# Hybrid decoder step on one core: transposes of short blocks take full 128x128 blocks

## The chip, the cores and the metric

The kernel runs on one core of one Trainium2 chip. The metric is the device time of one execution in microseconds (us), lower is better. Times of engines come from one profiled execution. PE is the tensor engine's matmul side, PEld its weight loads, DVE the vector engine, ACT the scalar engine, POOL GpSimd and SP the queue that issues most DMA transfers.

## What is computed

One layer of a decoder trunk, for a prompt of 1024 positions and for 8 samples of 8 positions each, 1088 rows in all, with 1024 channels, float32:

```python
h = rmsnorm(x, g_norm)
bg_a, cg_a, v_a, z_a, a_b, g_b, z_b, q_x, z_x = split(h @ w_in)        # 3200 columns
conv_a, new_ctx_a = causal_dwconv(ctx_a, cg_a * v_a, w_conv_a, b_conv_a)   # 3 taps, 384 channels
out_a = bg_a * conv_a * silu(z_a)
u_b = a_b * sigmoid(g_b)
conv_b, new_ctx_b = causal_dwconv(ctx_b, u_b, w_conv_b, b_conv_b)          # 31 taps, 384 channels
out_b = silu(layernorm(conv_b, ln_g, ln_b)) * silu(z_b)
out_x = cross_attn(q, mk, mv) * silu(z_x)                                  # 4 heads of 64, 256 memory tokens
y = rmsnorm(x + concat([out_a, out_b, out_x]) @ w_out, g_final)
```

The prompt's memory keys and values come from `rmsnorm(mem) @ w_mem_k` and `w_mem_v`; the samples bring theirs from a cache, and both bring conv states. Outputs are y, the new conv states of both convolutions, and the prompt's keys and values.

## The kernel before

Large products run in three passes of 32-bit matmuls over halves: each operand is split into a high and a low part (`hh`/`hl` for the activations, `wh`/`wl` for a weight tile), and a pass is high x high, low weight x high, high weight x low. The projection goes through 25 column tiles of 128 channels (`n`), each over three chunks of rows of 256, 384 and 448 (`CHUNKS`; the last has 384 rows of the prompt and the 64 of the samples). A pass is eight matmuls, one for each 128 channels of the input (`k`). After the third and the seventh matmul a queue of `steps` is served (`side`), and that is how all the other work of PE (transposes, attention, layer norm) gets between the passes. The taps of the long convolution are DVE instructions, placed behind the evacuations of the passes. Tiles in SBUF come from one pool (`B`), PSUM has four banks for the products (`MM`, names mm) and four for the rest (`SD`, names sd).

Within an engine the order is the order of the program as a scheduler laid it out before the run. The startup is an order written out by hand.

Transposes are PE instructions with the block as weights and the identity `ident` as the other operand; `tr(out, in_, n)` takes a block of n rows and the n x n corner of the identity. The places that the change touches:

- **x** (`x_load`, `x_tr`, `x_T`, `x_ev`): nine row tiles `xt` (names x) are loaded by SP, normalised in place and transposed; the ninth holds the samples and has 64 rows. `x_T(2, k)` makes the third chunk, for each of eight k: three blocks of 128x128 and the samples' block of 64 rows go to one sd bank, and from there ACT writes `hh` and DVE `hl`.
- **parameters and states** (`load_params`, `params_T`): 54 rows of parameters lie in `prow` (names prow), 120 rows of states in each of two `stb`; for each of three groups of channels one block of each is transposed.
- **new states** (`st_out`): 94 columns of `u_s` (names us) and 18 of `s_s` (names ss) are transposed, copied to SBUF and sent out by SP.
- **layer norm** (`ln_in`, `ln_sq`, `ln_scale`, `ln_out`): the convolution's output `accB` is transposed so that a row is a position (`lnx`), normalised, and transposed back; the ninth row tile is again that of the samples: on the way in 64 columns of 128 rows, on the way back 64 rows.
- **the startup**: POOL writes the zeros of `qblk` and then the identity. PE runs 12 matmuls on the identity as a warm-up (line 941, two records each), transposes the norm weights (`graw`, to `gT`), and then the first two row tiles of x, as soon as ACT and DVE have normalised them. ACT makes `hh` from these, piece by piece, and the first pass follows piece by piece, with more matmuls on the identity as fillers (line 972).

Of the kernel before, what the change touches and what calls it, by code (L numbers as in the profile page):

```python
# [11 lines left out]
AF = mybir.ActivationFunctionType  # L12
ALU = mybir.AluOpType
# [6 lines left out]
NS = 64  # L20
NT = SEQ + NS
# [14 lines left out]
def hybrid_trunk_kernel(  # L36
# [7 lines left out]
    nc = tc.nc  # L44
    S, G, T = nc.scalar, nc.gpsimd, nc.tensor
# [13 lines left out]
    V = Vector()  # L59
# [9 lines left out]
    def nm(s):  # L69
        uid[0] += 1  # L70
        return f"{s}_{uid[0]}"

    def B(s, dt=F32, cols=NT):
        return big.tile([128, cols], dt, tag="b", name=nm(s))

    def SD():
        return sdp.tile([128, 512], F32, tag="s", name=nm("sd"))
# [4 lines left out]
    def SM(s, cols):  # L82
        return sml.tile([128, cols], F32, tag=f"{s}{cols}", name=nm(s))

    pe_t, dve_t = [0.0], [0.0]
    steps, taps = deque(), deque()
# [8 lines left out]
    def tr(out, in_, n):  # L95
        T.transpose(out, in_, ident[:n, :n])  # L96
        pe_t[0] += 107

    def dv(ns):
        dve_t[0] += ns  # L100
# [22 lines left out]
        while steps:  # L123
            side()

# [8 lines left out]
    u_s = [cst.tile([128, 334], F32, name=f"us{j}") for j in range(3)]  # L134
# [17 lines left out]
        dv(800)  # L152
        return y0, t3

# [1 line left out]
    hh = [None] * KT  # L156
    hl = [None] * KT
    xt = [None] * 9
    xrows = [128] * 8 + [64]
    xcols = [i * 128 for i in range(9)]  # L160
    groups = [[0, 1], [2, 3, 4], [5, 6, 7, 8]]

    def x_src(i):
        return x_prompt[0, i * 128:(i + 1) * 128, :] if i < 8 else x_sample.rearrange("b t d -> (b t) d")

    def x_load(i):
        xt[i] = B("x", cols=D)
        nc.sync.dma_start(xt[i][:xrows[i]], x_src(i))

    class Norm:  # L170
# [28 lines left out]
    def x_T(c, k):  # L199
        x_ev(c, k, x_tr(c, k))  # L200

    def x_tr(c, k):
        off, n = CHUNKS[c]
        ps = SD()
        for i in groups[c]:
            o, r = xcols[i] - off, xrows[i]
            tr(ps[:, o:o + r], xt[i][:r, k * 128:(k + 1) * 128], r)
        return ps

    def x_ev(c, k, ps):  # L210
# [5 lines left out]
        )  # L216
        dv(n / 0.96 + 130)

# [1 line left out]
    order = (  # L220
        [("g", 0, 15), ("a", 0, 12), ("cg", 0, 3), ("v", 0, 6), ("bg", 0, 0)]
        + [("g", 1, 16), ("a", 1, 13), ("g", 2, 17), ("a", 2, 14)]
# [40 lines left out]
            wlo[n] = B("wl", F32R, D)  # L263
        split(whi[n], wlo[n], raw[n], half * 512, half * 512 + 512)

# [1 line left out]
    u_p = [None] * 3  # L267
    accB = [None] * 3
    W31, WA, BB, BA, LG, LB = 16, 47, 50, 51, 52, 53
# [43 lines left out]
                taps.append(mk(products, 16, 15))  # L313
        taps.append(total)

# [1 line left out]
    sig = [None] * 3  # L317
    s_p = [None] * 3
    cgt = [None]
# [159 lines left out]
        evac(n, c, ps)  # L479
        run_taps(taps_per(n))  # L480

# [1 line left out]
    stb = [None] * 2  # L483
    prw = [None]

    def load_params():
        q = nc.sync
        prow = prw[0] = B("prow", cols=384)
        q.dma_start(prow[0:16, :], state_conv_a[0].rearrange("b p c -> (b p) c"))
        q.dma_start(prow[W31:W31 + 31, :], w_conv_b[0])  # L490
        q.dma_start(prow[WA:WA + 3, :], w_conv_a[0])
        q.dma_start(prow[BB:BB + 1, :], b_conv_b)
        q.dma_start(prow[BA:BA + 1, :], b_conv_a)
        q.dma_start(prow[LG:LG + 1, :], ln_g)
        q.dma_start(prow[LB:LB + 1, :], ln_b)
        for h in range(2):
            stb[h] = B("stb", cols=384)
            q.dma_start(stb[h][:120], state_conv_b[0, 4 * h:4 * h + 4].rearrange("b p c -> (b p) c"))
        G.memset(qblk, 0.0)

    def params_T(j):
        ps = SD()
        cs = slice(j * 128, j * 128 + 128)
        tr(ps[:, 0:54], prw[0][:54, cs], 54)
        tr(ps[:, 64:184], stb[0][:120, cs], 120)
        tr(ps[:, 192:312], stb[1][:120, cs], 120)
        V.tensor_copy(prm[j], ps[:, 0:54])
        V.tensor_copy(
            s_s[j][:, 0:16].rearrange("p (t b) -> p b t", b=NB),
            ps[:, 0:16].rearrange("p (b t) -> p b t", b=NB),  # L510
        )
        for h in range(2):
            V.tensor_copy(
                u_s[j][:, 0:240].rearrange("p (t b) -> p b t", b=NB)[:, 4 * h:4 * h + 4],
                ps[:, 64 + 128 * h:184 + 128 * h].rearrange("p (b t) -> p b t", b=4),
            )
        dv(700)

# [1 line left out]
    mt = [None] * 2  # L520
    mT = {}
    wm = {}
# [86 lines left out]
        V.tensor_sub(KL[0][:, sl], ps, KH[0][:, sl].bitcast(F32))  # L609
        dv(600)  # L610

# [1 line left out]
    P_, PT, mx_, sm_ = {}, {}, {}, {}  # L613

    def at_scores(i):
# [58 lines left out]
    kc, vc, KTs, Os, Pts = {}, {}, {}, {}, {}  # L674

    def c_load(g, p):
# [73 lines left out]
                )  # L750
        dv(500)

# [1 line left out]
    def st_out():  # L754
        tb_ = B("ncb", cols=384)
        ta = B("nca", cols=384)
        ps = SD()
        for j in range(3):
            T.transpose(ps[:94, j * 128:j * 128 + 128], u_s[j][:, 240:334], ident)
        pe_t[0] += 321  # L760
        S.copy(tb_[:94], ps[:94, :384])
        ps = SD()
        for j in range(3):
            T.transpose(ps[:18, j * 128:j * 128 + 128], s_s[j][:, 64:82], ident)
        pe_t[0] += 321
        S.copy(ta[:18], ps[:18, :384])
        for t in range(8):
            nc.sync.dma_start(ncb_s[0, :, 22 + t, :], tb_[t * 8:t * 8 + 8])
        nc.sync.dma_start(ncb_s[0, :, 0:22, :], state_conv_b[0, :, 8:30, :])
        nc.sync.dma_start(ncb_p[0, 0], tb_[64:94])  # L770
        for t in range(2):
            nc.sync.dma_start(nca_s[0, :, t, :], ta[t * 8:t * 8 + 8])
        nc.sync.dma_start(nca_p[0, 0], ta[16:18])

# [1 line left out]
    lnx = {}  # L776
    lst = {}

    def ln_in(i):
        if i == 0:  # L780
            for s in ("sum", "sq"):
                lst[s] = SM(f"ln{s}", 9)
                G.memset(lst[s], 0.0)
        if i % 2 == 0:
            lnx[i // 2] = B("lnx", cols=768)
        r = xrows[i]
        ps = SD()
        for j in range(3):
            T.transpose(ps[:r, j * 128:j * 128 + 128], accB[j][:, i * 128:i * 128 + r], ident)  # L789
        pe_t[0] += 321  # L790
        S.activation(
            lnx[i // 2][:r, (i % 2) * 384:(i % 2) * 384 + 384], ps[:r, :384], AF.Copy,
            accum_out=lst["sum"][:r, i:i + 1],
        )

    def ln_mean():
# [2 lines left out]
        dv(100)  # L799

    def ln_sq(i):
        r = xrows[i]
        t = lnx[i // 2][:r, (i % 2) * 384:(i % 2) * 384 + 384]
        junk = SD()
        S.activation(junk[:r, :384], t, AF.Square, bias=lst["nmu"][:r, i:i + 1], accum_out=lst["sq"][:r, i:i + 1])

    def ln_rstd():
        y0, t3 = rstd_chain(lst["sq"], 9, 384)
# [1 line left out]
        V.tensor_tensor(lst["r"], y0, t3, ALU.mult)  # L810

    def ln_scale(i):
        r = xrows[i]
        t = lnx[i // 2][:r, (i % 2) * 384:(i % 2) * 384 + 384]
        V.tensor_scalar(t, t, lst["nmu"][:r, i:i + 1], lst["r"][:r, i:i + 1], ALU.add, ALU.mult)
        dv(330)

    def ln_out(j, g):
        ps = SD()
        n = 0  # L820
        for i in ((0, 1, 2, 3), (4, 5, 6, 7), (8,))[g]:
            r = xrows[i]
            tr(ps[:, n:n + r], lnx[i // 2][:r, (i % 2) * 384 + j * 128:(i % 2) * 384 + j * 128 + 128], r)
            n += r
        S.activation(
            accB[j][:, g * 512:g * 512 + n], ps[:, :n], AF.Silu,
            bias=prm[j][:, LB:LB + 1], scale=prm[j][:, LG:LG + 1],
        )

# [1 line left out]
    worder = [0, 1, 2, 6, 7, 3, 4, 5]  # L831
    wo_r, wo_h, wo_l = {}, {}, {}

# [86 lines left out]
    def startup():  # L920
# [3 lines left out]
        for i in (0, 1):  # L924
            x_load(i)
# [65 lines left out]
        n2.square(1)  # L991
        evac(2, 0, pr[2])
        t1 = [x_tr(1, k) for k in range(4)]
        pr = [MM(), MM(), MM()]
        for k in range(KT):
# [20 lines left out]
            evac(n, 1, pr[n])  # L1016
        flush_steps()

# [1 line left out]
    if True:  # L1020
        with tc.manual_schedule():
            startup()
        for n in range(0, NCT):
# [8 lines left out]
            kind, j, _ = order[n]  # L1032
# [47 lines left out]
            if n == 17:  # L1080
                ms[0] = B("ms", F32R, D)
                steps.append(st_out)
# [85 lines left out]
```

## Time and profile before

| what | value |
|---|---|
| time, median of 3 runs | 479.92 us (479.91 to 480.08) |
| span of the profiled execution | 479.3 us; its time outside the span is not listed, the median lies 0.6 us above |
| PE busy | 469.2 us, 98%, 2850 instructions |
| PEld busy | 428.5 us, 89% |
| DVE busy | 318.4 us, 66% |
| ACT busy | 221.9 us, 46% |
| POOL busy | 8.1 us, 2% |
| DMA | 40.42 MB, mean 84 GB/s |
| PE on the chain that ended last | 97% |

The busy time of PE includes matmuls whose ends are modelled, and successive ones overlap. A group of the timeline shows the start of its first instruction, the time to the end of its last, the engine, the line, the tiles (written <- read), the shape of the first and the number. The starts of two groups are the safer measure of what lay between.

### The profile page before, as it was taken

How to read it: one execution, taken by the hardware profiler on the slowest of the kernel's cores; microseconds unless marked ns; L12 is line 12 of the kernel's file. 1: busy time of each engine (PE TensorE's matmuls, PEld its weight loads, DVE VectorE, ACT ScalarE, POOL GpSimd, SP SyncE). 2: the span in 40 equal slices, each digit the busy share in tenths (PEclk: the TensorE clock that was granted, in tenths of full speed). 3: DMA queues.
4: the chain of work that ended last, by engine and by line, in shares of the span. 5: the costliest groups of instructions: out<-in, count | busy, mean ns of one | idle time of the engine just before them, and what ended most of it. 6: DMA issues, size and time to landing. Idle time of an engine off the chain costs nothing.

```text
span 479.3 us, 7262 instructions
## 1 busy us (share of the span) xinstructions
PE 469.2 (98%) x2850; PEld 428.5 (89%) x2850; DVE 318.4 (66%) x547; ACT 221.9 (46%) x573; POOL 8.1 (2%) x20
## 2 busy tenths in 40 slices
PE   7999999999999999999999999999999999999994
PEld 6998899999999999999999989899899888888884
DVE  4685599976958899798479598633563446333334
ACT  7874371250215349457592455558852433211111
POOL 2110000000000000000000000000000000000000
PEclk8999999999999999999999999999999999999998
DMA  9970221003440400111020521023401653211111
GB/s 284 353 236 1 89 88 45 0 1 90 130 132 1 133 0 1 46 44 46 2 74 15 176 88 30 17 58 100 166 0 46 189 228 110 87 45 44 45 59 72
DMA packets 39166, 40.42 MB, mean 84 GB/s; under 512 B 1647, under 2 KB 34325, under 8 KB 39125
## 3 DMA queue, kind: packets, MB, share of 16 engines
q1 hardware_dynamic: 39101, 39.96, 26.0%
q8 instruction: 22, 0.36, 0.3%
q14 instruction: 11, 0.09, 0.1%
q10 hardware_dynamic: 32, 0.01, 0.0%
HBM read 34.81 MB, written 5.42 MB: 84 GB/s over the span
## 4 chain that ended last, share of the span: by engine, by line
PE 97%; ACT 1%; DMA 1%; DVE 0%; issue 0%; DVEq 0%; ACTq 0%
PE mm L89 83%; PE sd L89 6%; PE sd L96 6%; DMA x<-in_x_prompt_dram 1%; PE sd L789 1%; ACT junk L180 0%; PE sd L972 0%; PE mm L96 0%; ACT x L191 0%; ACT y L141 0%; DVE yg L53 0%; ACT sd L899 0%; DVEq L1164 0%; DVE xres L53 0%; DVE t L53 0%
## 5 line engine op out<-in xcount | busy, mean ns | idle before, releaser
L89 PE MATMUL mm<-hh,wh 128*128 128x256 f32 (+2 forms) x600 | 119.4, 334 | 0.0
L89 PE MATMUL mm<-hl,wh 128*128 128x256 f32 (+2 forms) x600 | 117.2, 333 | 0.0
L53 DVE SCALAR_TENSOR_TENSOR accB<-u,prm,accB 128x1024 f32<-128x1024 f32 x90 | 115.3, 1282 | 1.5
L89 PE MATMUL mm<-hh,wl 128*128 128x256 f32 (+2 forms) x600 | 115.2, 331 | 0.0
L89 PEld LDWEIGHTS mm<-hh,wh 128*128 128x128 f32 x600 | 98.7, 190 | 4.9 <-issue 1.3
L89 PEld LDWEIGHTS mm<-hl,wh 128*128 128x128 f32 x600 | 97.8, 189 | 5.0 <-issue 1.3
L89 PEld LDWEIGHTS mm<-hh,wl 128*128 128x128 f32 x600 | 98.2, 189 | 4.0 <-issue 0.3
L89 PE MATMUL mm<-wol,mh 128*128 128x512 f32 (+1 forms) x136 | 51.4, 378 | 0.0
L89 PE MATMUL mm<-woh,mh 128*128 128x512 f32 (+1 forms) x136 | 51.3, 377 | 0.0
L89 PE MATMUL mm<-woh,ml 128*128 128x512 f32 (+1 forms) x136 | 51.3, 377 | 0.0
L53 DVE TENSOR_TENSOR xres<-mm,xres 128x512 f32<-128x512 f32 (+2 forms) x19 | 12.5, 662 | 39.8 <-PE mm L89 39.8
L869 ACT ACTIVATE sd<-xres 128x512 f32<-128x512 f32 (+1 forms) x16 | 9.6, 602 | 58.3 <-DVE xres L53 58.3
L53 DVE TENSOR_TENSOR wl<-wr,wh 128x512 fp32r<-128x512 f32 x50 | 33.4, 695 | 4.0 <-ACT wh L243 2.4
L89 PEld LDWEIGHTS mm<-woh,mh 128*128 128x128 f32 x136 | 25.6, 188 | 5.0 <-ACT woh L243 0.4
L89 PEld LDWEIGHTS mm<-wol,mh 128*128 128x128 f32 x136 | 25.6, 188 | 5.0 <-DVE wol L53 0.3
L89 PEld LDWEIGHTS mm<-woh,ml 128*128 128x128 f32 x136 | 25.6, 188 | 4.6
L243 ACT CAST wh<-wr 128x512 fp32r<-128x512 f32 x44 | 25.9, 621 | 0.0
L295 ACT ACTIVATE prod<-us,prm 128x64 f32<-128x64 f32 x93 | 23.6, 341 | 0.0
L636 ACT ACTIVATE P<-sd,nb 128x256 f32<-128x256 f32 x32 | 14.7, 473 | 16.5 <-DVE nb L53 16.4
L438 ACT ACTIVATE sz<-mm 128x256 f32<-128x256 f32 (+2 forms) x24 | 11.3, 472 | 22.9 <-PE mm L89 22.9
L338 ACT ACTIVATE sig<-mm 128x256 f32<-128x256 f32 (+2 forms) x6 | 2.8, 474 | 33.6 <-PE mm L89 33.6
L378 ACT CAST Q<-mm 64x384 fp32r<-64x384 f32 (+1 forms) x12 | 5.3, 439 | 23.6 <-PE mm L89 23.5
(188 smaller groups left out, 518.3 us busy)
## 6 DMA issues: line engine op xcount, KB each, us to landing
wr<-in_w_in_dram SPq DMA_DIRECT2D x25, 512.0 KB
x<-in_x_prompt_dram SPq DMA_DIRECT2D x8, 512.0 KB
wor<-in_w_out_dram SPq DMA_DIRECT2D x8, 512.0 KB
xres<-in_x_prompt_dram SPq DMA_DIRECT2D x8, 512.0 KB
out_dram<-xres SPq DMA_DIRECT2D x7, 512.0 KB
cache<-in_cache_mem_k_dram SPq DMA_DIRECT2D x8, 256.0 KB
cache<-in_cache_mem_v_dram SPq DMA_DIRECT2D x8, 256.0 KB
mem<-in_mem_prompt_dram SPq DMA_DIRECT2D x2, 512.0 KB
```

The source lines that it names most:

```text
L53: r = f(*a, **k)
L89: T.matmul(out, lhsT, rhs, start=start, stop=stop)
L96: T.transpose(out, in_, ident[:n, :n])
L243: S.copy(dst_hi[:, a:b], src[:, a:b])
L295: S.activation(p3[:, k, :], src, AF.Copy, scale=w[:, k0 + k:k0 + k + 1])
L338: S.activation(sig[j][:, off:off + n], ps[:, :n], AF.Sigmoid)
L378: S.copy(q[a, off:off + p], ps[a, :p])
L438: S.activation(sz[0][:, off:off + n], ps[:, :n], AF.Silu)
L636: S.activation(P_[i][:, h * 256:h * 256 + 256], bank[h // 2][:, (h % 2) * 256:(h % 2) * 256 + 256], AF.Exp, bias=nb[:, h:h + 1], scale=SCA ...
L789: T.transpose(ps[:r, j * 128:j * 128 + 128], accB[j][:, i * 128:i * 128 + r], ident)
L869: S.activation(junk[:rows], xr[:rows, cs], AF.Square, accum_out=ss[:rows, f:f + 1])
```

## The change

Every block that is transposed becomes 128 rows by 128 columns. Where there are fewer rows, the rest is zeros that POOL writes: rows 64 to 127 of the ninth x tile, all of prow ahead of its loads, rows 96 to 127 of the two stb tiles. Where there are fewer columns, neighbouring ones are taken: 128 columns of us from 206 on, so that the states stand 34 rows further down, and the last 128 columns of accB, so that the samples stand in rows 64 to 127 of the last layer-norm tile. The 18-column transposes of ss stay as they are, and so does the 16-row one of graw.

```diff
     def x_load(i):
         xt[i] = B("x", cols=D)
+        if xrows[i] < 128:
+            G.memset(xt[i][xrows[i]:], 0.0)
         nc.sync.dma_start(xt[i][:xrows[i]], x_src(i))
...
         for i in groups[c]:
-            o, r = xcols[i] - off, xrows[i]
-            tr(ps[:, o:o + r], xt[i][:r, k * 128:(k + 1) * 128], r)
+            o = xcols[i] - off
+            tr(ps[:, o:o + 128], xt[i][:, k * 128:(k + 1) * 128], 128)
...
         prow = prw[0] = B("prow", cols=384)
+        G.memset(prow, 0.0)
...
             stb[h] = B("stb", cols=384)
+            G.memset(stb[h][96:128], 0.0)
...
-        tr(ps[:, 0:54], prw[0][:54, cs], 54)
-        tr(ps[:, 64:184], stb[0][:120, cs], 120)
-        tr(ps[:, 192:312], stb[1][:120, cs], 120)
+        tr(ps[:, 0:128], prw[0][:, cs], 128)
+        tr(ps[:, 128:256], stb[0][:, cs], 128)
+        tr(ps[:, 256:384], stb[1][:, cs], 128)
...
-            T.transpose(ps[:94, j * 128:j * 128 + 128], u_s[j][:, 240:334], ident)
+            T.transpose(ps[:, j * 128:j * 128 + 128], u_s[j][:, 206:334], ident)
...
+    lncols = [i * 128 for i in range(8)] + [NT - 128]
...
-            T.transpose(ps[:r, j * 128:j * 128 + 128], accB[j][:, i * 128:i * 128 + r], ident)
+            T.transpose(ps[:, j * 128:j * 128 + 128], accB[j][:, lncols[i]:lncols[i] + 128], ident)
...
-        n = 0
-        for i in ((0, 1, 2, 3), (4, 5, 6, 7), (8,))[g]:
-            r = xrows[i]
-            tr(ps[:, n:n + r], lnx[i // 2][:r, (i % 2) * 384 + j * 128:(i % 2) * 384 + j * 128 + 128], r)
-            n += r
+        for n, i in enumerate(((0, 1, 2, 3), (4, 5, 6, 7), (8,))[g]):
+            o = (i % 2) * 384 + j * 128
+            tr(ps[:, n * 128:n * 128 + 128], lnx[i // 2][:, o:o + 128], 128)
+        src = ps if g < 2 else ps[:, 64:128]
+        n = 512 if g < 2 else NS
```

`ln_in`, `ln_sq` and `ln_scale` work on 128 rows of the ninth tile instead of 64, `ln_out` reads its silu's operand from `src`, and `st_out` copies and sends the shifted rows. Comments aside, that is all.

The order on PE is the same but for the shapes and one place below. In the third chunk of x, one group of four transposes (the last is the samples' tile) stands between matmuls of the third pass. Before:

```order
L89 MATMUL mm_396<-hl_148,wh_209 128x384
L96 MATMUL sd_522<-ident,x_108 128x128
L96 MATMUL sd_522<-ident,x_110 128x128
L96 MATMUL sd_522<-ident,x_112 128x128
L96 MATMUL sd_522<-ident,x_114 128x64
L89 MATMUL mm_396<-hl_150,wh_209 128x384
```

After:

```order
L89 MATMUL mm_400<-hl_152,wh_213 128x384
L96 MATMUL sd_526<-ident,x_108 128x128
L96 MATMUL sd_526<-ident,x_110 128x128
L96 MATMUL sd_526<-ident,x_112 128x128
L96 MATMUL sd_526<-ident,x_114 128x128
L89 MATMUL mm_400<-hl_154,wh_213 128x384
```

Nothing moved here; the fourth transpose writes 128 columns instead of 64.

On PE at the layer norm's way back, the transposes of the samples' tile (lnx) for the second and third group of channels stand between matmuls of the projection. Before:

```order
L96 MATMUL sd_3588<-ident,lnx_3417 128x64
L89 MATMUL mm_3638<-hh_155,wh_3440 128x384
L89 MATMUL mm_3638<-hh_141,wl_3441 128x384
L89 MATMUL mm_3638<-hh_143,wl_3441 128x384
L89 MATMUL mm_3638<-hh_145,wl_3441 128x384
L96 MATMUL sd_3591<-ident,lnx_3417 128x64
```

After:

```order
L96 MATMUL sd_3592<-ident,lnx_3421 128x128
L89 MATMUL mm_3642<-hh_159,wh_3444 128x384
L89 MATMUL mm_3642<-hh_145,wl_3445 128x384
L89 MATMUL mm_3642<-hh_147,wl_3445 128x384
L96 MATMUL sd_3595<-ident,lnx_3421 128x128
L89 MATMUL mm_3642<-hh_149,wl_3445 128x384
```

The third transpose moved one matmul ahead.

On POOL at the startup, from the first instruction of the kernel's own on (lnsum and lnsq are the layer norm's sums, ss those of the row norms). Before:

```order
L499 MEMSET qblk 128x512
masks.py:197 MEMSET ident 128x128
L783 MEMSET lnsum_3277 128x9
L783 MEMSET lnsq_3279 128x9
masks.py:199 ISA
masks.py:199 AFFINE_SELECT ident<-ident 128x128
L175 MEMSET ss_174 128x4
```

After:

```order
L789 MEMSET lnsum_3281 128x9
L789 MEMSET lnsq_3283 128x9
L169 MEMSET x_114 64x1024
L491 MEMSET prow_123 128x384
L501 MEMSET stb_132 32x384
L501 MEMSET stb_135 32x384
L503 MEMSET qblk 128x512
masks.py:197 MEMSET ident 128x128
masks.py:199 ISA
masks.py:199 AFFINE_SELECT ident<-ident 128x128
L177 MEMSET ss_178 128x4
```

The four new memsets and the two small ones stand ahead of the identity. On SP the order is the same; the first load into prow and the two loads into stb have POOL among what they wait for.

More of the change, by code (lines that the diff above doesn't have):

```diff
@@ L514, in params_T @@
                 u_s[j][:, 0:240].rearrange("p (t b) -> p b t", b=NB)[:, 4 * h:4 * h + 4],
-                ps[:, 64 + 128 * h:184 + 128 * h].rearrange("p (b t) -> p b t", b=4),
+                ps[:, 128 + 128 * h:248 + 128 * h].rearrange("p (b t) -> p b t", b=4),
             )
@@ L758, in st_out @@
         for j in range(3):
-            T.transpose(ps[:94, j * 128:j * 128 + 128], u_s[j][:, 240:334], ident)
+            T.transpose(ps[:, j * 128:j * 128 + 128], u_s[j][:, 206:334], ident)
         pe_t[0] += 321
-        S.copy(tb_[:94], ps[:94, :384])
+        S.copy(tb_, ps[:, :384])
         ps = SD()
@@ L767, in st_out @@
         for t in range(8):
-            nc.sync.dma_start(ncb_s[0, :, 22 + t, :], tb_[t * 8:t * 8 + 8])
+            nc.sync.dma_start(ncb_s[0, :, 22 + t, :], tb_[34 + t * 8:34 + t * 8 + 8])
         nc.sync.dma_start(ncb_s[0, :, 0:22, :], state_conv_b[0, :, 8:30, :])
-        nc.sync.dma_start(ncb_p[0, 0], tb_[64:94])
+        nc.sync.dma_start(ncb_p[0, 0], tb_[98:128])
         for t in range(2):
@@ L785, in ln_in @@
             lnx[i // 2] = B("lnx", cols=768)
-        r = xrows[i]
         ps = SD()
         for j in range(3):
-            T.transpose(ps[:r, j * 128:j * 128 + 128], accB[j][:, i * 128:i * 128 + r], ident)
+            T.transpose(ps[:, j * 128:j * 128 + 128], accB[j][:, lncols[i]:lncols[i] + 128], ident)
         pe_t[0] += 321
         S.activation(
-            lnx[i // 2][:r, (i % 2) * 384:(i % 2) * 384 + 384], ps[:r, :384], AF.Copy,
-            accum_out=lst["sum"][:r, i:i + 1],
+            lnx[i // 2][:, (i % 2) * 384:(i % 2) * 384 + 384], ps[:, :384], AF.Copy,
+            accum_out=lst["sum"][:, i:i + 1],
         )
@@ L801, in ln_sq @@
     def ln_sq(i):
-        r = xrows[i]
-        t = lnx[i // 2][:r, (i % 2) * 384:(i % 2) * 384 + 384]
+        t = lnx[i // 2][:, (i % 2) * 384:(i % 2) * 384 + 384]
         junk = SD()
-        S.activation(junk[:r, :384], t, AF.Square, bias=lst["nmu"][:r, i:i + 1], accum_out=lst["sq"][:r, i:i + 1])
+        S.activation(junk[:, :384], t, AF.Square, bias=lst["nmu"][:, i:i + 1], accum_out=lst["sq"][:, i:i + 1])
     def ln_rstd():
@@ L812, in ln_scale @@
     def ln_scale(i):
-        r = xrows[i]
-        t = lnx[i // 2][:r, (i % 2) * 384:(i % 2) * 384 + 384]
-        V.tensor_scalar(t, t, lst["nmu"][:r, i:i + 1], lst["r"][:r, i:i + 1], ALU.add, ALU.mult)
+        t = lnx[i // 2][:, (i % 2) * 384:(i % 2) * 384 + 384]
+        V.tensor_scalar(t, t, lst["nmu"][:, i:i + 1], lst["r"][:, i:i + 1], ALU.add, ALU.mult)
         dv(330)
@@ L819, in ln_out @@
         ps = SD()
-        n = 0
-        for i in ((0, 1, 2, 3), (4, 5, 6, 7), (8,))[g]:
-            r = xrows[i]
-            tr(ps[:, n:n + r], lnx[i // 2][:r, (i % 2) * 384 + j * 128:(i % 2) * 384 + j * 128 + 128], r)
-            n += r
+        for n, i in enumerate(((0, 1, 2, 3), (4, 5, 6, 7), (8,))[g]):
[3 more added lines that the diff above has]
+        n = 512 if g < 2 else NS
         S.activation(
-            accB[j][:, g * 512:g * 512 + n], ps[:, :n], AF.Silu,
+            accB[j][:, g * 512:g * 512 + n], src, AF.Silu,
             bias=prm[j][:, LB:LB + 1], scale=prm[j][:, LG:LG + 1],
```

## The prediction

> **What bounds the kernel now.** I read the page first: the busy shares and the chain that ended last.
>
> ```profile
> span 479.3 us, 7262 instructions
> PE 469.2 (98%) x2850; PEld 428.5 (89%) x2850; DVE 318.4 (66%) x547; ACT 221.9 (46%) x573; POOL 8.1 (2%) x20
> PE 97%; ACT 1%; DMA 1%; DVE 0%; issue 0%; DVEq 0%; ACTq 0%
> ```
>
> PE is on the chain for 97% of the span, so whatever PE spends after the first ten microseconds or so counts in full, and nothing that another engine saves counts by itself. A busy PE is not a fast PE, though: a matmul that starts late behind a weight load is still drawn as busy. So I read next the groups kept apart by shape, for the weight loads of the transposes (after the bar: busy us, mean ns of one; then the idle time ahead of them).
>
> ```profile
> L96 PEld LDWEIGHTS sd<-ident,mem 128*128 128x128 f32 x16 | 1.9, 140 | 0.1
> L96 PEld LDWEIGHTS sd<-ident,x 64*128 64x128 f32 x8 | 1.1, 135 | 1.3 <-issue 1.2 <-DVE y L53 0.2
> ```
>
> A load of 64 rows lasts about as long as a full one (135 against 140 ns), but ahead of each stand 0.17 us in which the weight path waits for nothing that the profile shows ("issue"); sixteen full ones have 0.1 us in all. What such a pause costs I take from the timeline of PE: from one row's start to the start of a later one is what PE really spent on the work between.
>
> ```profile
> 24.33 0.49 PE L96 MATMUL sd<-ident,x 128*128 128x128 f32 x3
> 24.58 0.78 PE L89 MATMUL mm<-hh,wh 128*128 128x384 f32 x3
> 25.19 0.49 PE L96 MATMUL sd<-ident,x 128*128 128x128 f32 x3
> ...
> 28.48 4.32 PE L89 MATMUL mm<-hh,wl 128*128 128x384 f32 x24
> 32.63 0.86 PE L89 MATMUL mm<-hl,wh 128*128 128x384 f32 x4
> 33.33 0.69 PE L96 MATMUL sd<-ident,x 128*128 128x128 f32 x4
> ...
> 38.31 1.37 PE L96 MATMUL sd<-ident,x 128*128 128x128 f32 x8
> 39.61 0.97 PE L89 MATMUL mm<-hl,wh 128*128 128x384 f32 x4
> 40.43 0.69 PE L96 MATMUL sd<-ident,x 128*128 128x128 f32 x4
> 41.05 0.97 PE L89 MATMUL mm<-hl,wh 128*128 128x384 f32 x4
> 41.86 0.69 PE L96 MATMUL sd<-ident,x 128*128 128x128 f32 x4
> ```
>
> A 384-column matmul costs (32.63 - 28.48) / 24 = 0.173 us. Three full transposes with three matmuls take 25.19 - 24.33 = 0.86, so 0.34 for the three, 0.11 each and 0.44 for four. Three full blocks and one of 64 rows with four matmuls take 41.86 - 40.43 = 1.43, so 1.43 - 0.69 = 0.74: **0.30 us more with one short block**, although it moves half the columns. (The timeline merges the shapes; the fourth of each x4 is the short one.) Two such groups in a row take 40.43 - 38.31 - 0.69 = 1.43 against 0.88, 0.55 more.
>
> **Samples' rows of x.** Eight groups carry the samples' block: two pairs and four single groups, 2 x 0.55 + 4 x 0.30 = 2.3 us, all on PE, which go if a padded block behaves like the other full ones. What is late next is the bank: four PSUM banks serve the groups, and the fifth needs the first one back from DVE.
>
> ```profile
> 36.59 2.45 DVE L53 SCALAR_TENSOR_TENSOR hl<-sd,gT,hh 128x448 fp32r<-128x448 f32 x4
> ```
>
> Group one starts at 33.33; with 0.44 for a group and 0.69 for the matmuls between (four groups, three sets), the fifth would start at 33.33 + 3.83 = 37.16 and the sixth, right behind, at 37.6. DVE comes to this row from other work without a gap, so PE can't hurry it; one of its four takes 0.61, and banks come free at 37.2 and 37.8. That takes back 0.05 + 0.2: **2.05 us saved**.
>
> **States and parameters.**
>
> ```profile
> 45.12 0.26 PE L96 MATMUL sd<-ident,prow 54*128 54x54 f32 x1
> ...
> 49.49 0.27 PE L96 MATMUL sd<-ident,prow 54*128 54x54 f32 x1
> ...
> 50.78 1.81 PE L89 MATMUL mm<-hh,wl 128*128 128x448 f32 x8
> 52.43 1.81 PE L89 MATMUL mm<-hl,wh 128*128 128x448 f32 x8
> ```
>
> From one group of three transposes to the next stand eight matmuls, which take 52.43 - 50.78 = 1.65. Two rounds last 49.49 - 45.12 = 4.37, so a group costs 4.37 / 2 - 1.65 = 0.53, against 3 x 0.11. Three groups save 3 x 0.2 = **0.6 us**. The loads into prow and stb now wait for POOL's zeros, written by 4 us (below); SP comes to these loads later than that, behind its x, w and mem loads, so nothing behind them in its queue loses time.
>
> **Layer norm, the way back.**
>
> ```profile
> 345.16 0.27 PE L96 MATMUL sd<-ident,lnx 64*128 64x64 f32 x1
> 345.37 0.45 PE L89 MATMUL mm<-hh,wh 128*128 128x384 f32 x1
> 345.65 0.70 PE L89 MATMUL mm<-hh,wl 128*128 128x384 f32 x3
> 346.28 0.27 PE L96 MATMUL sd<-ident,lnx 64*128 64x64 f32 x1
> ```
>
> One 64-row transpose with four matmuls takes 346.28 - 345.16 = 1.12, less 0.69 is 0.43: 0.3 more than a full one; three of them, 0.9. ACT has to give back their banks, and the third now stands one matmul earlier on PE, with ACT busy just then; for that I take off 0.1, half a matmul: **0.8 us saved**.
>
> **Blocks short in columns, not in rows** (the last of accB, 64 columns of 128 rows; the states out, 94 columns).
>
> ```profile
> 325.77 0.49 PE L789 MATMUL sd<-ident,accB 128*128 128x128 f32 x3
> ...
> 327.06 0.49 PE L789 MATMUL sd<-ident,accB 128*64 128x128 f32 x3
> ...
> 328.33 1.55 PE L89 MATMUL mm<-hh,wh 128*128 128x384 f32 x8
> ```
>
> Three full ones and eight matmuls take 1.29, three short ones and eight matmuls 1.27: no pause to remove, 0.02 to lose. The same is assumed for the 94 columns. The wider ACT and DVE instructions cover more partitions with as many elements in each. All of this I cost at **nothing**; it would be hidden by PE anyway, which waits for none of it.
>
> **The start.** This is the cost.
>
> ```profile
> 0.73 0.52 POOL L499 MEMSET qblk<- 128x512 f32 x1 [0.29 <-POOLq L1155]
> 1.19 0.20 POOL masks.py:197 MEMSET ident<- 128x128 f32 x1
> ```
>
> A memset costs 0.83 ns a column and 0.09 us (0.52 for 512, 0.20 for 128). Zeros of 1024, 384, 384 and 384 columns ahead of the identity are 0.95 + 3 x 0.41 = 2.2 us, so PE's warm-up, which waits for the identity, starts near 4.0 instead of 1.85.
>
> ```profile
> 1.85 4.47 PE L941 MATMUL sd<-ident 128*128 128x128 f32 x24 [1.85 <-POOL ss L175]
> ...
> 8.22 0.68 PE L96 MATMUL sd<-ident,x 128*128 128x128 f32 x3 [1.73 <-ACT x L191]
> 8.69 0.85 PE L96 MATMUL mm<-ident,x 128*128 128x128 f32 x3
> 9.33 0.85 PE L96 MATMUL sd<-ident,x 128*128 128x128 f32 x3
> ...
> 13.86 0.36 PE L89 MATMUL mm<-hh,wl 128*128 128x256 f32 x1
> ```
>
> ```profile
> 9.79 1.20 ACT L212 ACTIVATE hh<-sd,gT 128x256 fp32r<-128x256 f32 x3 [0.59 <-PE sd L96]
> ```
>
> ```profile
> 5.08:8.49 3.41, 1.68 (x14) 1.46 (x14) 2.30 (x12) 3.35 (x8) 0.00 (x0) 1.00 1.16 308
> 8.49:11.91 3.42, 3.42 (x19) 3.42 (x17) 3.42 (x8) 2.83 (x8) 1.68 (x2) 0.50 1.13 350
> ```
>
> In the windows (length, then busy times from PE to POOL, then the granted clock) the clock is full from 5.08 to 8.49, and half from 8.49 to 11.91, after a stretch with PE busy for only 1.68 of 3.41 us. If the clock steps at the same places, the late warm-up runs at half clock, (9.33 - 8.69) / 3 = 0.213 a piece, up to 8.49, where 21 of 24 are done, and ends near 8.8; the transpose of g follows and the first x comes near 9.1 instead of 8.2, now without PE's gap of 1.7, so the full clock should stay. The seventh transpose of x, for which ACT waits, then starts at 9.1 + 6 x 0.11 = 9.8 instead of 9.33 and, by the 0.46 from there to ACT's start less what the full clock gains, ACT begins near 10.1 instead of 9.79. Its eight pieces of 0.40 end at 13.3, and PE follows with one matmul and two fillers of about 0.11 each: the second pass starts near 13.8, where it now starts at 13.86, since PE worked off a backlog made at half clock. Bounds: 2.2 lost, if the delay passes through whole; 0.6 gained, ACT's idle time in the row at 9.79, if the clock rises early enough that ACT has nothing to wait for. I take **0.1 lost**: nearest to the row at 13.86, and on the side of a loss, since POOL's memsets may also wait for each other.
>
> The Trainium skill ("TensorE: Matmul & The Clock Gate", Part 1) has the clock decided in free-running windows of about 3.4 us, with half clock after an idle one. The trace agrees on the length (3.41 and 3.42), but here the clock fell after a window that was half busy.
>
> **Sum.** 2.05 + 0.6 + 0.8 - 0.1 = 3.35 us. The profiled span of 479.3 becomes 475.95. The median of the runs, 479.92, lies 0.6 above that span, so the forecast is 476.6. A measurement of this kernel tells about 0.2%, 0.96 us, from no change.
>
> **Rivals.**
>
> A. The start's delay passes through: whole, 3.45 - 2.2 = 1.25 saved, 478.7; half, 2.35 saved, 477.6. For it: PE did wait 1.85 us for POOL. Against it: PE's gap of 1.73 ahead of the first x takes up most of it.
>
> B. Other engines take back gain further on: PE waits for nothing there now, so their margins aren't seen. Half lost, 478.2. Against it: DVE is busy for 66% and ACT for 46%, and what waits for PE moves forward with it.
>
> C. Slower: the late warm-up leaves the clock low. Each further window of 3.4 us at half clock costs PE 1.7; with the 2.2 passing whole, two of them cost 5.6 against 3.45, so 482.1. It is slower from a loss of 4.4 on. Against it: PE no longer has the gap after which the clock fell.
>
> D. The pause isn't made by the missing rows but by the change from one kind of work to another, and stays. Then nothing is saved, and with 0.1 lost the time is 480.0. For it: 135 against 140 ns, rows don't shorten a load. Against it: the mem groups change kind as often and don't pause.
>
> The Trainium skill, same page ("LDWEIGHTS (loading the stationary operand)"), says that a load's time goes by its columns and not by its rows: by that rule alone D holds, and padding can't save anything. The trace agrees for the load itself and shows the pause outside it.
>
> **Chances.** The forecast case 0.72, with its own range from 475.6 (0.6 gained at the start, and 0.3 of the 0.35 taken off for banks doesn't come) to 477.2 (0.7 lost at the start). A 0.11, B 0.09, D 0.04, C 0.04, half of it no change and half slower. Faster by over 0.2% are the forecast, A and B, 0.92; no change D and half of C, 0.06; slower 0.02. The range reaches from 475.5 into A and B, to 478.3; A's upper end, C and D are left out.
>
> **What the profile after would show.** The "issue" ahead of the samples' and parameters' weight loads is gone; the last of the eight groups starts near 40.1 (41.86 now); a parameter group with its eight matmuls takes 1.98 and not 2.19; the warm-up starts near 4.0 and the second pass between 13.7 and 14. The prediction is wrong if the pauses are still there, if the second pass starts after 15, or if DVE or ACT stands as PE's releaser after 40 us with more than 0.5 us.

## The result, and the profile after

| kernel | median, us | lowest to highest | ratio to before |
|---|---|---|---|
| before | 479.92 | 479.79 to 480.08 | 1 |
| after | 477.75 | 476.93 to 478.50 | 0.995 (0.9933 to 0.9966) |

The change saves 2.17 us by the medians, and 1.6 to 3.2 us by the interval. The forecast was 476.6, with 475.5 to 478.3 as its range. The page of after, to set beside the first lines of the prediction:

```profile
span 476.7 us, 7269 instructions
PE 465.8 (98%) x2850; PEld 427.6 (90%) x2850; DVE 318.3 (67%) x547; ACT 221.8 (47%) x573; POOL 10.3 (2%) x24
```

PE executes as many instructions as before and is busy for 3.4 us less; POOL has four memsets and 2.2 us more. This span belongs to an execution of 478.50 us, so 1.8 us lie outside the span. All later profiles have the same 1.8.

The groups of weight loads by shape (after the bar: busy us, mean ns of one; then idle time ahead of them):

```profile
L96 PEld LDWEIGHTS sd<-ident,x 128*128 128x128 f32 x66 | 7.8, 144 | 1.2 <-DVE hl L53 0.7
L96 PEld LDWEIGHTS sd<-ident,prow 128*128 128x128 f32 x3 | 0.4, 139 | 0.0
```

The "issue" is gone from both. What idle time is left ahead of the x loads ends mostly with DVE's `hl`, 0.7 us. Of that 0.5 us lies here, on the timeline of the weight loads:

```profile
38.27 0.42 PEld L96 LDWEIGHTS sd<-ident,x 128*128 128x128 f32 x4 [0.31 <-DVE hl L53]
38.86 0.42 PEld L96 LDWEIGHTS sd<-ident,x 128*128 128x128 f32 x4 [0.17 <-DVE hl L53]
```

These are the fifth and the sixth group, which wait for the banks that the prediction named. On PE's timeline (start, time to the end of the last, engine, line, operation, tiles, shape of the first, count), the third chunk of x and the parameter groups:

```profile
34.26 0.60 PE L96 MATMUL sd<-ident,x 128*128 128x128 f32 x4
34.62 0.95 PE L89 MATMUL mm<-hl,wh 128*128 128x384 f32 x4
...
36.20 0.94 PE L89 MATMUL mm<-hl,wh 128*128 128x384 f32 x4
...
37.34 0.94 PE L89 MATMUL mm<-hl,wh 128*128 128x384 f32 x4
38.27 1.25 PE L96 MATMUL sd<-ident,x 128*128 128x128 f32 x8
39.27 0.94 PE L89 MATMUL mm<-hl,wh 128*128 128x384 f32 x4
40.06 0.60 PE L96 MATMUL sd<-ident,x 128*128 128x128 f32 x4
...
41.19 0.60 PE L96 MATMUL sd<-ident,x 128*128 128x128 f32 x4
41.55 1.87 PE L89 MATMUL mm<-hh,wh 128*128 128x448 f32 x8
...
44.07 0.27 PE L96 MATMUL sd<-ident,prow 128*128 128x128 f32 x1
...
47.98 0.27 PE L96 MATMUL sd<-ident,prow 128*128 128x128 f32 x1
...
49.12 1.78 PE L89 MATMUL mm<-hh,wl 128*128 128x448 f32 x8
50.74 1.78 PE L89 MATMUL mm<-hl,wh 128*128 128x448 f32 x8
```

A single group with its four matmuls takes 41.19 - 40.06 = 1.13 instead of 1.43, and less 0.69 for the matmuls 0.44: the length of four full blocks. Four matmuls and a pair of groups behind them take 36.20 - 34.62 = 1.58 at the second and third group, which wait for no bank, and 39.27 - 37.34 = 1.93 at the fifth and sixth: the banks cost PE 0.35. Two parameter rounds take 47.98 - 44.07 = 3.91, 1.96 each.

What each stage gained, by the starts on PE at its two ends:

| stage | before | after | saved |
|---|---|---|---|
| third chunk of x: first group to the 448-column pass | 33.33 to 42.48 | 34.26 to 41.55 | 1.86 |
| parameters: that pass to the next `mm<-hh,wl` pass | 42.48 to 50.78 | 41.55 to 49.12 | 0.73 |
| states out (us) to the first lnx block on the way back | 312.27 to 339.72 | 310.44 to 337.89 | 0.00 |
| layer norm, way back, to the pass behind it | 339.72 to 347.47 | 337.89 to 344.90 | 0.74 |
| second pass to PE's last matmul | 13.86 to 472.56 | 14.80 to 470.01 | 3.49 |

The last row is what I call the body: 458.70 before, 455.21 after. The 3.49 is the gain behind the start, and the forecast had 3.45.

The four stages above it add up to 3.33. The other 0.16 lies in the five 448-column passes behind the parameters, which hold no transpose: a pass takes 50.74 - 49.12 = 1.62 in after and 52.43 - 50.78 = 1.65 in before (rows in the prediction). The runs below show these two paces and none between: the five passes take 8.27 in before, e2, e5, e8 and e9, and 8.11 in all others. As e6 keeps every short block and has 8.11, and e8 pads x and has 8.27, the 0.16 doesn't follow the pauses. Nothing in the traces says what sets the pace; where bodies are compared below, the 0.16 is named.

The median gained only 2.17. The rest went in the start:

```profile
0.93 0.95 POOL L169 MEMSET x<- 64x1024 f32 x1
1.94 0.42 POOL L491 MEMSET prow<- 128x384 f32 x1
2.42 0.77 POOL L501 MEMSET stb<- 32x384 f32 x2
...
3.71 0.21 POOL masks.py:197 MEMSET ident<- 128x128 f32 x1
4.34 5.49 PE L944 MATMUL sd<-ident 128*128 128x128 f32 x24 [4.34 <-POOL ss L177]
9.97 0.74 PE L96 MATMUL sd<-ident,x 128*128 128x128 f32 x3
...
14.80 1.20 PE L89 MATMUL mm<-hh,wl 128*128 128x256 f32 x8
```

The identity comes after four memsets, the warm-up starts at 4.34 instead of 1.85, and its 24 records take 5.49 us, 0.23 a piece, near the 0.213 that the prediction read at half clock. By the trace's clock records the clock is full from 10.42, and the second pass starts at 14.80. With the predicted 13.8 that is a loss of 1.0, but the runs below show that the row I measured it against, 13.86, was itself not the usual start of before.

The theory after this: short blocks of rows cost a pause, padding removes it, and the zeros cost part of that gain because they stand ahead of the identity. Rivals: the pause belongs to the change of kind of work; a shorter block costs in proportion to its missing rows, or once for each short block; and the lost microsecond is not the zeros' but chance, or the fault of a warm-up that queues ahead of x.

### The profile page after: what moved, and what is told of

Read it like the earlier page. It is cut to its first block, busy times and chain, and to the rows that moved or that the text cites. A ratio compares the mean times of both kernels' runs of the same rounds, so it can differ in the third digit from the quotient of the medians.

```text
span 476.7 us, 7269 instructions
## 1 busy us (share of the span) xinstructions
PE 465.8 (98%) x2850; PEld 427.6 (90%) x2850; DVE 318.3 (67%) x547; ACT 221.8 (47%) x573; POOL 10.3 (2%) x24
## 3 DMA queue, kind: packets, MB, share of 16 engines
q1 hardware_dynamic: 39101, 39.96, 26.7%
## 4 chain that ended last, share of the span: by engine, by line
PE 97%; DVE 1%; POOL 1%; issue 0%; ACT 0%; DVEq 0%; POOLq 0%; ACTq 0%
PE mm L89 83%; PE sd L89 6%; PE sd L96 5%; PE sd L944 1%; PE sd L794 1%; DVE wl L53 0%; PE sd L975 0%; POOL x L169 0%; POOL stb L501 0%; DVE yg L53 0%; ACT sd L902 0%; POOL qblk L503 0%; DVEq L1167 0%; DVE xres L53 0%; POOL prow L491 0%
## 5 line engine op out<-in xcount | busy, mean ns | idle before, releaser
L640 ACT ACTIVATE P<-sd,nb 128x256 f32<-128x256 f32 x32 | 14.8, 473 | 16.5 <-DVE nb L53 16.4
```

Of the source, the lines that this page charges most:

```text
L640: S.activation(P_[i][:, h * 256:h * 256 + 256], bank[h // 2][:, (h % 2) * 256:(h % 2) * 256 + 256], AF.Exp, bias=nb[:, h:h + 1], scale=SCA ...
```

## Experiments

Kernels timed together share their runs of before. Its median was 480.32 beside the first four runs named e1 to e4, 479.91 beside e5 to e9, and 480.43 beside e10 to e12; e5 to e9 ran on another chip than the other experiments. Two profiles of one kernel agree within 0.05 in the body (458.70 and 458.75 before, 455.21 and 455.17 after), so a single profile is enough to read it.

**The gain without the zeros ahead: the identity first (e1).** On the kernel after, in the startup:

```diff
+        make_identity(nc, ident)
         ...
         w_load(4)
-        make_identity(nc, ident)
```

> The changed kernel with the identity written ahead of POOL's zeros; nothing else. Theory (the padded blocks save 3.3 us on PE, the zeros ahead of the identity give about 0.9 back at the start, more or less by where the clock steps): the warm-up starts near 1.5, the second pass (first matmul with a low weight) near 13.8 instead of 14.80, and the time is 476.4 to 476.8, about 1.0 below the changed kernel's 477.75, with a spread of runs below 0.6. Rival (the gain was lost further on, behind 40 us): the start is earlier but the time stays at 477.4 to 478.

Measured: 476.94 (476.27 to 479.48), ratio 0.9937 (0.9918 to 0.9956). The profiled execution has a span of 474.5:

```profile
1.39 5.01 PE L944 MATMUL sd<-ident 128*128 128x128 f32 x24 [1.39 <-POOL ident masks.py:199]
...
12.60 1.19 PE L89 MATMUL mm<-hh,wl 128*128 128x256 f32 x8
```

The second pass starts at 12.60, 2.2 earlier than in after, and the body is 455.19, as in after. In this profile the same zeros, written behind the identity, cost nothing: the second pass starts as early as it does without them in e5 (12.64), though here the warm-up also starts 0.46 earlier than in before. By the times this is less sure, since the interval of the ratio overlaps that of after (0.9933 to 0.9966). The median came out somewhat above what was expected, and the spread of 3.2 far above. Of its six executions the three with a mean granted clock of 0.995 to 0.999 lie at 476.27 to 476.41, and the three with 0.991 to 0.993 at 477.46 to 479.48. In the profiles a mean of 0.993 or 0.994 goes with a clock that fell back to half in the start (the first of before, and e12), and all others have 0.995 or more. So the clock of the start is the likely cause; it is not shown, as the last three left no trace.

**The cost alone: zeros written, blocks left short (e2).** On the kernel before, the four memsets of the change and nothing else:

```diff
+        if xrows[i] < 128:
+            G.memset(xt[i][xrows[i]:], 0.0)
...
+        G.memset(prow, 0.0)
...
+            G.memset(stb[h][96:128], 0.0)
```

> The kernel before with the four memsets of zeros where the change puts them; every transpose stays as it was. Theory: the warm-up starts near 4.3, the clock rises late by an amount that differs from run to run, the time is 480.2 to 481.6, the median about 0.9 above before. Rival A (the delay is hidden by the wait for x): 479.9, second pass at 13.9. Rival C (the clock stays low for whole windows more): above 482.

Measured: 481.55 (480.71 to 481.87), ratio 1.002 (1.0006 to 1.0033): slower by 1.2 us.

```profile
4.34 5.49 PE L945 MATMUL sd<-ident 128*128 128x128 f32 x24 [4.34 <-POOL ss L177]
...
14.50 0.72 PE L89 MATMUL mm<-hh,wl 128*128 128x256 f32 x4
```

The start of after with the body of before: 473.25 (PE's last matmul) - 14.50 = 458.75. The start's loss comes with the zeros, then, whatever the blocks are: 1.2 us by the medians, 0.3 to 1.6 by the interval.

**One part alone: x (e3).** On the kernel before, x in full blocks, with its one memset behind the identity:

```diff
-            o, r = xcols[i] - off, xrows[i]
-            tr(ps[:, o:o + r], xt[i][:r, k * 128:(k + 1) * 128], r)
+            o = xcols[i] - off
+            tr(ps[:, o:o + 128], xt[i][:, k * 128:(k + 1) * 128], 128)
...
+        G.memset(xt[8][64:], 0.0)
```

> The kernel before with the samples' x block padded alone, and its zeros written behind the identity, so that the start stays. Theory (a pause for every block of fewer rows): the eight groups save 1.8 to 2.1 us, 477.9 to 478.1. Rival (the pause comes with the change of work and not with the rows): 479.9.

Measured: 478.42 (477.72 to 479.02), ratio 0.9961 (0.9949 to 0.9972). The stage of the third chunk, from the first group to the 448-column pass:

```profile
32.69 0.60 PE L96 MATMUL sd<-ident,x 128*128 128x128 f32 x4
...
39.96 1.87 PE L89 MATMUL mm<-hh,wh 128*128 128x448 f32 x8
```

It takes 39.96 - 32.69 = 7.27 instead of 9.15 (42.48 - 33.33): 1.88 saved, against 2.05 in the prediction. The body is 456.62, 2.08 less than 458.70, but 0.16 of that is the other pace of the five passes behind the parameters. The time is somewhat above what was expected: the second pass began at 13.21 in the profiled execution.

**Before, once more (e5).** The kernel before without an edit, for a second profile.

> The kernel before, unchanged, for a span and a time of the same execution. Theory (the first profile of before fell on an execution in which the clock dropped for a window, and the time lies 1.8 us above the span as in the other runs): time less span is 1.7 to 1.9; if the clock doesn't drop in this one, the second pass starts at 12.7 to 13.2 and the span is about 478.2; if it does, 13.9 and 479.3. From the second pass's start to the last matmul's it takes 458.7 either way. Rival (the start is always as in the first profile): time less span 0.6, second pass at 13.9, span 479.3.

Measured: 479.90, the median of before.

```profile
span 478.1 us, 7262 instructions
...
8.09 0.55 PE L96 MATMUL sd<-ident,x 128*128 128x128 f32 x3 [1.00 <-ACT x L191]
...
12.64 1.20 PE L89 MATMUL mm<-hh,wl 128*128 128x256 f32 x8
```

The windows of this execution and of the one that the prediction read (length, then busy us and count from PE to POOL, the granted clock, the share and GB/s of DMA):

```profile
9.00:12.00 3.00, 2.98 (x25) 2.55 (x23) 3.00 (x8) 2.95 (x10) 1.38 (x2) 1.00 1.11 356
```

```profile
9.00:12.00 3.00, 3.00 (x16) 3.00 (x15) 3.00 (x7) 2.41 (x7) 1.68 (x2) 0.52 1.12 363
```

With the clock full, the second pass of before starts at 12.64, not at 13.86. This execution is a usual one: of the 17 of before that were timed beside e5 to e9, twelve took 479.84 to 479.93. Other kernels with the same early warm-up and a clock that stayed full have 12.56, 12.79 and 13.21 (e8, e6, e3). The first profile belonged to an execution in which the clock fell back to half; by the 1.8 us outside the span it took 481.1 and not 479.9. Against 12.64 the start of after loses 2.16 in its profile.

**After, once more (e11).** The kernel after without an edit.

> The changed kernel, unchanged, for a second profile. Theory (its start differs from run to run with the place at which the clock steps, the rest doesn't): warm-up at 4.34 again, clock up somewhere between 7 and 10.5, second pass at 13.2 to 14.9, and from there to the last matmul 455.2 as in the first profile. Rival (the spread of 1.6 between its runs lies elsewhere): the second pass within 0.2 of 14.80 and a different time behind it.

Measured: 477.75, and its body 455.17.

```profile
4.34 5.02 PE L944 MATMUL sd<-ident 128*128 128x128 f32 x24 [4.34 <-POOL ss L177]
...
14.09 1.08 PE L89 MATMUL mm<-hh,wl 128*128 128x256 f32 x7
```

The same start at 4.34, but the clock is full from 8.73 instead of 10.42, and the second pass starts at 14.09: 1.45 behind the 12.64 of before. The two profiled executions of after differ in their starts and in nothing behind them.

**A shorter warm-up (e10).** If the late warm-up delays x by standing ahead of it in PE's queue, half as many should help. On the kernel after:

```diff
-    WARM = 12
+    WARM = 6
```

> The changed kernel with 6 warm-up matmuls instead of 12; the zeros stay ahead of the identity. Theory (the delay costs because the late warm-up, at half clock, keeps PE until 9.5 while x is ready at 8): six end near 7, x starts at 8.0 to 8.2, the second pass between 12.6 and 13.9, and the time is 476.3 to 477.5, below the changed kernel's 477.75. Rival (what costs is the clock's late rise, whatever stands in PE's queue): with fewer warm-up matmuls the clock rises later still, the second pass starts at 14 to 15, 477.7 to 478.7.

Measured: 477.95 (477.66 to 478.34), ratio 0.994 (0.9923 to 0.9958). No better than the 477.75 of after beside it.

```profile
4.34 2.93 PE L944 MATMUL sd<-ident 128*128 128x128 f32 x12 [4.34 <-POOL ss L177]
8.13 0.90 PE L96 MATMUL sd<-ident,x 128*128 128x128 f32 x3 [0.64 <-ACT x L193]
...
14.22 0.96 PE L89 MATMUL mm<-hh,wl 128*128 128x256 f32 x6
```

The first x comes at 8.13, as early as in before, so the queue is out of the way. But x then runs at half clock (0.90 for three against 0.55 in e5), the clock is full only from 12.53, and the second pass starts at 14.22. My theory of the queue fell: without the queue the loss stayed. The run changed two things at once, the queue and the place where the clock steps up, so that the late clock is the loss is what fits the starts and not shown by itself.

**A longer warm-up on the early start (e4).** e1 with this:

```diff
-    WARM = 12
+    WARM = 20
```

> The identity first, and 20 warm-up matmuls instead of 12, so that PE has no gap ahead of the first x and the clock doesn't fall again. Theory (the clock falls after a window with PE half busy): the granted clock stays full from its first rise on, the second pass starts at 13.3 to 13.7, and the time is 0.2 to 0.6 below that of the identity first with 12, 475.9 to 476.5. Rival (ACT's pieces set the start, not the clock): the same time as with 12, within 0.2. Against both: if the clock rises late, 20 matmuls end after the first x is ready, and it gets up to 0.5 slower.

Measured: 476.74 (476.44 to 477.11), ratio 0.9926 (0.9914 to 0.9937): the lowest median of all versions, 3.6 us under the before beside it, and with a spread of 0.7 instead of e1's 3.2. Its highest time is below the median of after, though the intervals of the two ratios still touch (0.9914 to 0.9937 and 0.9933 to 0.9966).

```profile
1.39 6.65 PE L944 MATMUL sd<-ident 128*128 128x128 f32 x40 [1.39 <-POOL ident masks.py:199]
8.24 0.55 PE L96 MATMUL sd<-ident,x 128*128 128x128 f32 x3
...
12.79 1.20 PE L89 MATMUL mm<-hh,wl 128*128 128x256 f32 x8
```

The warm-up now ends at 8.04, as x arrives, so PE has no gap there, and the clock stays full, as the theory had it. The second pass starts at 12.79; I had expected 13.3 or later. The time is above the expected 475.9 to 476.5, and 0.2 below e1, which the rival allowed too: the runs don't tell 20 from 12 here by the time.

**The longer warm-up on before (e9).** `WARM = 20` on the kernel before, with the identity where it stood.

> The kernel before with 20 warm-up matmuls instead of 12. Theory (part of before's spread is a clock that drops after the gap ahead of the first x): no drop, the second pass at 12.7 to 13.3, the time 479.8 to 480.4 with a spread below 0.8, so the median stays where it is and the slow executions go. Rival (the drop doesn't matter): same median and the same spread of 1.2 and more.

Measured: 480.72 (479.93 to 481.51), ratio 1.0012 (1.0003 to 1.0022): no gain, rather 0.6 us worse by the ratio, with a spread of 1.6.

```profile
1.85 6.74 PE L941 MATMUL sd<-ident 128*128 128x128 f32 x40 [1.85 <-POOL ss L175]
8.69 0.55 PE L96 MATMUL sd<-ident,x 128*128 128x128 f32 x3
...
13.15 1.20 PE L89 MATMUL mm<-hh,wl 128*128 128x256 f32 x8
```

From 1.85 the forty records end at 8.59, so the first x waits, at 8.69 instead of 8.09, and the second pass starts at 13.15 instead of 12.64. The clock didn't fall back, but the spread stayed, and the median rose: the theory that a longer warm-up helps by itself fell. That it helps beside the earlier identity rests on the spreads of e1 and e4, six and five executions, and isn't shown.

**What makes the pause: each short block, or the change to it (e6).** On the kernel before, each short block of x is transposed twice, one behind the other:

```diff
             tr(ps[:, o:o + r], xt[i][:r, k * 128:(k + 1) * 128], r)
+            if r < 128:
+                tr(ps[:, o:o + r], xt[i][:r, k * 128:(k + 1) * 128], r)
```

> The kernel before with the samples' 64-row transpose of the third chunk issued twice in a row in each of the eight groups. Theory (a pause for every short block): the second one costs 0.20 as the first does, so the work from the second pass on takes 1.6 more, 460.3. Rival (a pause at the change between full and short): the second one costs 0.11, 0.9 more in all, 459.6.

Measured: 480.34 once, body 459.06, 0.36 more than before. The five passes behind the parameters run at the faster pace here and hide 0.16, so the stage itself is the measure:

```profile
32.28 0.75 PE L96 MATMUL sd<-ident,x 128*128 128x128 f32 x5
...
41.93 1.89 PE L89 MATMUL mm<-hh,wh 128*128 128x448 f32 x8
...
L96 PEld LDWEIGHTS sd<-ident,x 64*128 64x128 f32 x16 | 1.6, 137 | 1.3 <-issue 1.2 <-DVE y L53 0.2
```

The last line is from the groups by shape, the others from PE's timeline. The stage takes 41.93 - 32.28 = 9.65 instead of 9.15: 0.06 for each of eight added blocks, below what either theory had (0.20 and 0.11). Sixteen loads have the same 1.2 us of "issue" in all as eight had. The single starts of the last group show where the pause stands. The first short block starts 0.20 behind the full one ahead of it, where full blocks follow each other in 0.11; the second starts 0.11 behind the first. In before, the next matmul starts 0.20 behind the short block, in after 0.03 behind the full one in its place. The theory that every short block pauses fell: the pauses stand at the two changes, into a block of 64 rows and out of it, and a second block of 64 rows behind the first has none ahead of it. The "issue" of the weight path shows only the first of the two; the 0.30 that the prediction read on PE holds both.

**How short is short (e8).** On the kernel before, the samples' block with 96 rows, 32 of them zeros written behind the identity:

```diff
             o, r = xcols[i] - off, xrows[i]
+            r = max(r, 96)
...
+        G.memset(xt[8][64:], 0.0)
```

> The kernel before with the samples' block padded to 96 rows and 96 columns instead of 128 (zeros behind the identity). Theory (every block of fewer than 128 rows pauses): as with 64 rows, 458.7 from the second pass on. Rival (only blocks up to half the rows pause): as with 128 rows, 456.6 as in the run with the x block padded alone.

Measured: 477.91 once. The stage takes 39.34 - 32.03 = 7.31, 1.84 less than before, and the body of 456.86 is 1.84 less too.

```profile
L96 PEld LDWEIGHTS sd<-ident,x 96*128 96x128 f32 x8 | 1.1, 140 | 0.0
...
L96 PEld LDWEIGHTS sd<-ident,prow 54*128 54x128 f32 x3 | 0.4, 135 | 0.9 <-issue 0.9
```

In one kernel, 96 rows have no idle time ahead and 54 rows have 0.3 us each. It isn't "fewer than 128 rows" either: 96 rows do as well as 128, 7.31 against the 7.27 of e3. (The bodies differ by 0.24, of which 0.16 is the pace of the five passes.)

**The parameters alone (e12).** On the kernel before with the identity first, only prow padded; the two blocks of states keep their 120 rows (the identity's move and the copies' new columns are not printed):

```diff
+        G.memset(prow, 0.0)
...
-        tr(ps[:, 0:54], prw[0][:54, cs], 54)
-        tr(ps[:, 64:184], stb[0][:120, cs], 120)
-        tr(ps[:, 192:312], stb[1][:120, cs], 120)
+        tr(ps[:, 0:128], prw[0][:, cs], 128)
+        tr(ps[:, 128:248], stb[0][:120, cs], 120)
+        tr(ps[:, 256:376], stb[1][:120, cs], 120)
...
```

> The kernel before with the block of parameters alone padded, 54 rows to 128 (identity first, zeros behind it); the state blocks keep their 120 rows. Theory (only blocks of up to half the rows pause): all of that group's gain comes, 0.7, so 458.0 from the second pass to the last matmul. Rival (120 rows pause too): half of it or less, 458.4 or more.

Measured: 480.02 once, body 457.85.

```profile
L96 PEld LDWEIGHTS sd<-ident,stb 120*128 120x128 f32 x6 | 0.8, 140 | 0.2
L96 PEld LDWEIGHTS sd<-ident,prow 128*128 128x128 f32 x3 | 0.4, 138 | 0.0
...
42.29 1.90 PE L89 MATMUL mm<-hh,wh 128*128 128x448 f32 x8
...
49.88 1.79 PE L89 MATMUL mm<-hh,wl 128*128 128x448 f32 x8
```

The parameter stage takes 49.88 - 42.29 = 7.59, in after 7.57, before 8.30. All of that stage's gain came from the 54-row block; padding the 120-row blocks of states brought nothing. The body is 0.85 less than before, 0.71 by this stage and the rest by the pace of the five passes. This execution was one in which the clock fell back: full from 5.24 to 8.65, then half to 12.07, and its second pass starts at 13.68, just like the first profile of before.

## Why the prediction was right, and where it wasn't

**Samples' rows of x: right.** Predicted 2.05, measured 1.86 in the stage, and 1.88 for this part alone (e3). The wait for banks is there, at the fifth and sixth groups as predicted; it cost 0.35 where 0.25 was taken off. That the body's 3.49 lies so close to the 3.45 of the forecast is in part luck: 0.16 of it is the pace of five passes, which the prediction didn't have.

**States and parameters: right in size, not in attribution.** Predicted 0.6, measured 0.73. The three blocks of a group were costed together; e12 shows that the 54-row block carries all of it.

**Layer norm: right.** Predicted 0.8, measured 0.74.

**Short columns: right.** Predicted nothing, and the stage from the states out to the way back takes 27.45 us in both kernels.

**The start: mis-sized.** The term was 0.1 lost. Measured are 1.45 and 2.16 in two profiles of after against 12.64, and 3.49 - 2.17 = 1.3 by the medians. (Beside e10 and e11 before has a median of 480.43 and after is 2.7 faster in one execution, which leaves 0.8; e2 has 1.2.) Three things went into it. The row at 13.86 was taken as the usual start of before; it was one with the clock fallen back, and the usual start is 12.64 (e5). The clock was assumed to step up where it did in that profile; after a warm-up from 4.34 it stepped up at 10.42 and 8.73 (10.17 in e2). And the memsets with the gaps between them delayed the warm-up to 4.34, not to 4.0. The warm-up then ended at 9.83 and the first x came at 9.97, against 8.8 and 9.1 in the forecast.

**"The median lies 0.6 above that span": wrong.** Time outside the span is 1.8 us in every run with both numbers. The first profile's span of 479.3 belongs to an execution of 481.1. This error and the one in the start have one cause, a profile taken as typical, and partly cancel: the sum off the span, 475.95, is 0.75 below the profiled 476.7, and with 1.8 instead of 0.6 it would have given 477.75, the measured median, by luck. From the typical profile of before, span 478.1 and second pass at 12.64, the same terms with the start at 13.8 give 478.1 - 3.45 + 1.16 = 475.8, and 477.6 with what lies outside.

**The rivals.** A is what happened, in its half version (477.6): about half of the 2.2 us came through. B did not happen: the body kept its 3.49. C did not happen: the highest time of after is 478.50, and the clock came late but stayed. D was half right in its mechanism and wrong in its result: the pause does stand at a change, but at the change between 64-row and full loads, so full blocks do away with it (e3, e6, e8). The loads themselves last 135 ns with 54 rows, 137 with 64, 140 with 96 and 139 with 128. In this the trace agrees with the rule of the Trainium skill that the prediction set beside D ("TensorE: Matmul & The Clock Gate", "LDWEIGHTS (loading the stationary operand)"); the pause stands outside the load, where that rule says nothing.

**What the profile after was to show.** The "issue" is gone; a parameter round takes 1.96 (forecast 1.98). The last of the eight groups starts at 41.19 instead of 40.1, of which the later start (14.8 for 13.8) is 1.0. The second pass at 14.8 was outside 13.7 to 14, though not after 15. Neither DVE nor ACT is a releaser of PE after 40 us; the 0.5 at 38.27 and 38.86 is the wait for banks.

**What is left open.** What it is in the change from 64 rows to full ones that pauses: nothing in the trace names it, and no run had between 65 and 95 rows. Nor did any run take rows and columns apart: a transpose of n rows reads an n x n corner of the identity, so a short block always wrote few columns too, and a pause made by these would look the same. The Trainium skill ("TensorEngine Tiling (Array Packing)", "Tiling Modes" with its "Key Properties") has the array work as tiles of 128, 64 or 32 rows and drain when that mode changes. The runs fit this for rows: 54 and 64 rows pause (1.2 us in 8 loads of 64), 96 and 120 do not (0.0 in 8 loads, 0.2 in 6), and a second short block pauses no more (e6). They don't fit it for columns, where the same section has modes of 128 x 64 too, if a block with 64 columns of weights counts as one: the three accB blocks with 64 columns of weights cost 1.27 with their eight matmuls, against 1.29 for full ones. The prediction did not use this rule; it would have named the change, and the gain would have been the same. That the start's loss is 1.3 by the medians and up to 2.16 in one profile is put down to where the clock steps up, from two profiles of after; it wasn't set from outside.

## What to carry to other kernels

Look at the idle time ahead of small weight loads before padding anything: here padding paid only for blocks of up to 64 rows between full ones, 0.3 us of PE for each, and padding those of 120 rows, or of fewer columns, brought nothing. Put what padding needs (the zeros) behind the work that the first PE instruction waits for: the same four memsets cost 1.2 us ahead of the identity (e2), and behind it nothing that the profile of e1 shows. Profile the kernel before twice if its first microseconds matter, check that the profiled execution's time is the median's, and compare stage by stage: the totals of two kernels can differ by something that the change wasn't made for, here 0.16 us.

## What the runs showed of the hardware

Where the clock steps up varies from run to run of the same start. With the warm-up from 1.85 it was full from 5.08, 5.33, 6.10, 6.35, 6.88 and 7.34 in six profiles. They lie within 2.26 us, less than the 3.41 of one window; that fits the free-running windows of the Trainium skill ("TensorE: Matmul & The Clock Gate", Part 1).

It can fall back after one window in which PE is busy for about half. In the first profile of before and in that of e12, PE was busy for 1.68 of the first 3.41 us at full clock, and half clock followed; e6 with 1.77, e1 with 1.95, and e3, e4, e5, e8 and e9 with 2.39 to 3.41 kept it. Where the gap ahead of x falls in that window would then decide whether an execution loses a microsecond. Filling the gap kept the clock full in e4 and e9, but only e4 has a small spread of times (0.7, against 1.6 in e9), so the gap isn't all that makes executions differ. These are nine profiles and not a set threshold.

These are the windows of e12 and e6, with the columns as above:

```profile
5.24:8.65 3.41, 1.68 (x14) 1.46 (x14) 2.62 (x14) 3.35 (x8) 0.00 (x0) 1.00 1.17 309
8.65:12.07 3.42, 3.42 (x19) 3.42 (x18) 3.42 (x9) 3.09 (x8) 1.72 (x2) 0.50 1.12 353
```

```profile
5.33:8.74 3.41, 1.77 (x16) 1.55 (x16) 2.53 (x13) 3.34 (x9) 0.00 (x0) 1.00 1.17 309
```
